# Low parts of every second mixer weight by an adding DMA in SBUF, with larger background budgets

## Chip, cores and metric

One core of a Trainium2 chip runs the kernel. The metric is the device time of one execution in microseconds (us), from runs without a profile; one more execution was profiled.

## What is computed

Two layers over 272 tokens (16 learned meta tokens and 256 inputs) of width 1024, all in float32:

```python
for l in range(DEPTH):
    h = h + 0.5 * swiglu(rmsnorm(h, g_ffn1[l]), w1_gate[l], w1_up[l], w1_down[l])
    n = rmsnorm(h, g_mix[l])
    z = n @ w_in[l]                      # u, q, k, v, f_logit, gates
    y_a = s5_mixer(u, ...)               # state space branch: a scan over time, 32 groups of 64 states
    y_b = forgetting_attention(q, k, v, f_logit + b_f[l])
    merged = gates[..., :D_MODEL] * (y_a @ w_br_a[l]) + gates[..., D_MODEL:] * (y_b @ w_br_b[l])
    h = h + merged @ w_o[l]
    h = h + 0.5 * swiglu(rmsnorm(h, g_ffn2[l]), w2_gate[l], w2_up[l], w2_down[l])
return rmsnorm(h[:, N_META:], g_final)
```

## The kernel before, in words

**Weights.** All weights stream from HBM once, as 378 units of 128 rows, most of them 1024 columns wide (512 KB). A product must keep float32's precision, so a weight w is split into a high part (w rounded to fp32r) and a low part (w minus the high part), and so is the activation. `unit` (L289 to L300) issues three matmuls for each of the 8 slices of a unit: high by high (L298), high by low activation (L299), low by high activation (L300). `load` (L138) issues the load from the SP queue into one of 4 `raw` buffers; `high` (L148) makes the high part on ScalarE (ACT) with the cast of L158, in one of 5 `wh` buffers; `low` (L162) makes the low part on VectorE (DVE) with the subtraction of L171, in one of 4 `wl` buffers.

**Order of the work.** The order on every engine is that in which the program issues instructions; nothing reorders it. `tick` (L264) is called after each unit. It calls `high` for the unit four ahead, then whatever is due (`due`: evictions, splits and copies registered with `later`), then `low` for the unit three ahead, then `background`. `group` (L302) does the first units of a stage a slice at a time and calls `high` and `low` inside. `background` (L252) runs a generator of small DVE operations, each with a price in the code's own nanoseconds, until the tick's budget is spent; a price that overshoots is paid back in the next ticks:

```python
state["credit"] = min(state["credit"], 0.0) + state["budget"]
while g is not None and (all_of_it or state["credit"] > 0):
    c = next(g, None)
    ...
        state["credit"] -= c
```

`finish_background` (L281) issues all that is left at once. In the first feed-forward block the generator is `ssm_setup` and `ssm_tables(0)` (the tables E and Cx, L601 to L633), begun 8 ticks into the block and finished at L1293 before the mixer starts; in the second one it is `ssm_tables(1)`; in a mixer it is `ssm_branch` (L638), finished at L1111.

**The mixer.** It takes 53 units, counted here from 0: units 0 to 3 give u, 4 (narrow, 256 columns) the forget gate, 5 to 8 v, 9 to 12 k, 13 to 16 q, 17 to 32 the gates with the attention between them, 33 and 34 the first half of the attention branch's projection, 35 to 38 the GLU of the state space branch, 39 to 44 the rest of both branches' projections, 45 to 52 the output projection. The budget is QKV_BUDGET in the ticks of units 0 to 16, GATE_BUDGET or LATE_BUDGET afterwards, FFN_BUDGET after L1111.

`have_u` (L757) scales a block of u, splits it and calls `done` (L761): 12 DMA copies from SBUF to SBUF, each of 32 rows and 34 KB, issued from the GpSimd (POOL) queue at L765, which lay the parts out for the matmul `bu` of the branch (L645). The ticks order them so: the copies of u's blocks 0 and 1 (24) are issued in the tick after unit 3, just ahead of `low` for unit 6; those of block 2 in the next tick, ahead of `low` for unit 7; those of block 3 in the one after, ahead of `low` for unit 8. The POOL queue holds these copies, the two memsets of L745 and little else. The state space branch's operations on DVE are products with the table E (L667), adds (L720, L722) and scans (L732); PE then forms the output with L657.

Of the kernel before, what the change touches and what calls it, by code (L numbers as in the profile page):

```python
# [7 lines left out]
F32 = mybir.dt.float32  # L8
F32R = mybir.dt.float32r
I32 = mybir.dt.int32  # L10
AF = mybir.ActivationFunctionType
ALU = mybir.AluOpType
# [4 lines left out]
D = 1024  # L17
KD = D // P
# [4 lines left out]
NF = DFF // P  # L23
DEPTH = 2
# [5 lines left out]
LEAD = 4  # L30
RAW = 4
SMALL = 200
FFN_BUDGET = 900.0
QKV_BUDGET = 1600.0
GATE_BUDGET = 2700.0
LATE_BUDGET = 2600.0
EARLY_B = 2
# [2 lines left out]
WARM = 10  # L40
START = 8
BLOCK = 1024
BROWS = 96
DELAY = 2
MASKED = -float(2.0 ** 100)
# [34 lines left out]
def plan():  # L80
    units = layer_units() * DEPTH
    blocks, where, off = [], [], 0
    for i, w in enumerate(units):
        if i > 4 and blocks and blocks[-1][1] + w <= BLOCK:
            blocks[-1][1] += w
        else:
            blocks.append([off, w])
        where.append((len(blocks) - 1, blocks[-1][1] - w, w))
        off += w
    return blocks, where, off  # L90


BLOCKS, WHERE, NCOL = plan()
# [36 lines left out]
class Weights:  # L130
# [7 lines left out]
    def load(self):  # L138
        if self.nb >= len(BLOCKS):
            return  # L140
        off, w = BLOCKS[self.nb]
        t = self.pool.tile([P, BLOCK], F32, tag="raw", name=f"raw{self.nb}", bufs=RAW)
        src = self.dram[off * P : (off + w) * P].rearrange("(p n) -> p n", p=P)
# [4 lines left out]
    def high(self, parts=1):  # L148
# [10 lines left out]
        self.part[i] = (hi, r)  # L159
        self.nh += 1  # L160

    def low(self, parts=1):  # L162
        i, nc = self.nl, self.nc
        if i >= len(WHERE):
            return
        w = WHERE[i][2]
        hi, r = self.part[i]
        lo = self.pool.tile([P, D], F32R, tag="wl", name=f"wl{i}", bufs=LEAD)
        for c in range(0, w, w // parts):
            k = slice(c, c + w // parts)  # L170
            nc.vector.tensor_sub(lo[:, k], r[:, k], hi[:, k].bitcast(F32))  # L171
        self.part[i] = (hi, lo)
        self.nl += 1
# [7 lines left out]
def body(tc, nc, ins, out):  # L181
    v, s, pe = nc.vector, nc.scalar, nc.tensor

    with (
# [49 lines left out]

        state = {"tick": 0, "bg": None, "credit": 0.0, "budget": FFN_BUDGET}
        queue, tails, mids = [], [], []
# [39 lines left out]
        def flush():  # L276
            due(10**9)
            while tails:
                tails.pop(0)()

        def finish_background():  # L281
            while state["bg"] is not None or mids:
                background(True)
                for fn in [mids.pop(0) for _ in range(len(mids))]:
                    fn()
                due(state["tick"] + 1)
# [26 lines left out]
        def split(hi, lo, x, then=None, when=None):  # L313
            s.copy(hi, x)  # L314

            def low():
                v.tensor_sub(lo, x, hi.bitcast(F32))
                if then is not None:
                    then()

            if when is None:
                later(1, low)
            else:
                when(low)


        def norm_in(d, gname, l, hh, hl, t0):

            x, g = h[:, d, t0:], pc(gname, l, d)
            a, b = hh(d)[:, t0:], hl(d)[:, t0:]  # L330
            s.activation(a, x, AF.Copy, scale=g)  # L331

            def low():
                v.scalar_tensor_tensor(b, x, g, a.bitcast(F32), ALU.mult, ALU.subtract)  # L334

            later(1, low)
# [197 lines left out]
        E = cp.tile([P, 2, NJ, TS + 1], F32, name="E")  # L534
        Bs = cp.tile([BROWS, NJ, 2 * P], F32R, name="Bs")
        Cx = cp.tile([P, 4, NJ, 32], F32, name="Cx")

        def ssm_tables(l):

            js = slice(l * NJ, (l + 1) * NJ)  # L540
            top = BROWS - 32
            for j in range(0, NJ, 4):
                x = Bs[:, j : j + 4].rearrange("p j c -> p (j c)")
                slots = halves.take(), halves.take(F32R)
                raw, hi = (y.rearrange("p a t -> p (a t)")[:BROWS, : 8 * P] for y in slots)
                nc.sync.dma_start(raw, ins["B"][l][:, j * 2 * P : (j + 4) * 2 * P])
# [91 lines left out]
        def ssm_branch(l, us, yr, t0):  # L638
            n = T - t0

            def bu(j):
                pb = bp.tile([P, 2, 512], F32, tag="b2", name=f"bu{next(names)}")
                m, q = divmod(j, 4)
                for r in range(2):
                    pe.matmul(pb[:, r, :T], lhsT=Bs[:, j, r * P : r * P + P], rhs=us[m](q)[:BROWS], start=True, stop=True)  # L645
                if q == 3:
# [94 lines left out]
        def mixer(l, hh, hl, t0, finish):  # L741
# [33 lines left out]
            state["bg"] = ssm_branch(l, us, yr, t0)  # L775
            state["budget"] = QKV_BUDGET
            for m in range(4):
# [333 lines left out]
            finish_background()  # L1111
            state["budget"] = FFN_BUDGET
            flush()
# [295 lines left out]
def _ssm_mats(inp):  # L1409
    B = np.zeros((DEPTH, 32, 4, 4, 2, P), np.float32)  # L1410
    C = np.zeros((DEPTH, P, 2, NJ, 32), np.float32)
    for r, (kb, kc) in enumerate((("ssm_b_re", "ssm_c_re"), ("ssm_b_im", "ssm_c_im"))):
        for gi in range(2):
# [3 lines left out]
            C[:, gi * 64 : gi * 64 + 64, r, :, gi * 16 : gi * 16 + 16] = c.transpose(0, 3, 1, 2)  # L1417
    return np.concatenate([B.reshape(DEPTH, 32, -1)] * (BROWS // 32), axis=1), C

# [27 lines left out]
```

## Time and profile before

| what | us |
|---|---|
| median of 3 runs (1238.59 to 1239.59) | 1239.27 |
| the profiled execution, whole | 1240.03 |
| its span, first to last instruction | 1238.2 |
| PE busy / DVE busy / ACT busy / POOL busy in the span | 1196.4 / 937.1 / 645.1 / 53.1 |

PE is TensorE's matmuls, PEld its weight loads, SPq the queue that issues the weight loads from HBM. "A <- B" behind a row's numbers names what ended a wait. Busy PE means that a matmul was in flight by modelled ends. PEclk is the granted TensorE clock, 1.00 for the upper of its two levels (2.4 GHz) and 0.50 for the lower (1.2 GHz). The first mixer lies at about 208 to 431 us of the span, the second at about 831 to 1040 us.

### The profile page before, as it was taken

What the parts mean: (1) busy time and instruction counts of PE and PEld (TensorE: products, weight loads), DVE (VectorE), ACT (ScalarE), POOL (GpSimd) and SP (SyncE); (2) the same over time, 40 slices, a digit from 0 to 9 for tenths busy, and PEclk for the clock granted to TensorE, in tenths of its full rate; (3) what the DMA queues carried; (4) which work ended last, traced back from release to release, by engine and by line L of the source; (5) the groups of instructions that cost most, each with busy time, mean ns of one, the idle gap of its engine ahead of it and who ended that gap; (6) DMA issues with size and microseconds to landing.
All of it is one profiled execution on the core that took longest, in us unless ns stands there. A gap on an engine that the chain in (4) does not pass through costs nothing.

```text
span 1238.2 us, 24127 instructions
## 1 busy us (share of the span) xinstructions
PE 1196.4 (97%) x9753; PEld 1170.0 (94%) x9753; DVE 937.1 (76%) x1722; ACT 645.1 (52%) x1052; POOL 53.1 (4%) x108
## 2 busy tenths in 40 slices
PE   9999999889979999999999999999999899999997
PEld 8999999788869999999999999999888699999997
DVE  7976888899997867888765555557998897756553
ACT  7556444536646665444454444446374576544542
POOL 0000000420000000000000000006100000000000
PEclk9999999899999999999999999999999899999999
DMA  7766554553334657655556555546432345655561
GB/s 243 208 194 202 183 176 137 171 160 116 93 99 133 188 179 228 181 175 166 174 171 185 178 172 166 176 156 207 154 103 87 102 154 172 225 185 186 175 186 64
DMA packets 60159, 204.71 MB, mean 165 GB/s; under 512 B 7920, under 2 KB 8304, under 8 KB 60048
## 3 DMA queue, kind: packets, MB, share of 16 engines
q1 hardware_dynamic: 56480, 199.06, 51.7%
q0 software_dynamic: 3152, 3.50, 0.9%
q8 instruction: 76, 1.25, 0.4%
q10 hardware_dynamic: 416, 0.62, 0.1%
q14 instruction: 35, 0.29, 0.1%
HBM read 198.75 MB, written 1.05 MB: 161 GB/s over the span
## 4 chain that ended last, share of the span: by engine, by line
PE 88%; DVE 9%; issue 2%; DMA 1%; ACT 0%; SPq 0%; DVEq 0%; ACTq 0%
PE ps L298 28%; PE ps L300 28%; PE ps L299 28%; DVE wl L171 2%; PE ps L657 2%; DVE m L667 1%; DVE g L732 1%; DVE p L667 1%; PE bu L645 1%; DMA raw<-wts 1%; PE ps L965 0%; DVE p L722 0%; DVE p L720 0%; PE ps L1030 0%; DVE mx L975 0%
## 5 line engine op out<-in xcount | busy, mean ns | idle before, releaser
L300 PE MATMUL ps<-m,wl 128*128 128x272 f32 (+2 forms) x2960 | 851.8, 288 | 6.3 <-DVE wl L171 6.3
L298 PE MATMUL ps<-m,wh 128*128 128x272 f32 (+2 forms) x2960 | 855.4, 289 | 0.8 <-ACT m L1064 0.5
L299 PE MATMUL ps<-m,wh 128*128 128x272 f32 (+2 forms) x2960 | 848.8, 287 | 0.1
L158 ACT CAST wh<-raw 128x1024 fp32r<-128x1024 f32 (+2 forms) x380 | 388.5, 1025 | 428.0 <-issue 222.5
L300 PEld LDWEIGHTS ps<-m,wl 128*128 128x128 f32 (+1 forms) x2960 | 558.8, 189 | 7.2 <-DVE wl L171 7.0
L298 PEld LDWEIGHTS ps<-m,wh 128*128 128x128 f32 (+1 forms) x2960 | 558.9, 189 | 5.6 <-issue 3.6
L299 PEld LDWEIGHTS ps<-m,wh 128*128 128x128 f32 (+1 forms) x2960 | 558.6, 189 | 1.0 <-DVE m L334 0.5
L171 DVE TENSOR_TENSOR wl<-raw,wh 128x1024 fp32r<-128x1024 f32 (+2 forms) x380 | 450.3, 1186 | 55.1 <-PE ps L300 38.9
L391 DVE TENSOR_TENSOR t<-t,ps 128x272 f32<-128x272 f32 (+1 forms) x88 | 38.1, 433 | 78.6 <-PE ps L300 76.2
L385 DVE TENSOR_TENSOR t<-ps,rstd 128x272 f32<-128x272 f32 (+1 forms) x88 | 38.3, 436 | 47.7 <-PE ps L300 47.2
L765 POOL DMA_DIRECT2D m<-m x96 | 47.2, 497 | 47.3 <-ACT m L314 32.9
L667 DVE TENSOR_TENSOR p<-bu,E 128x544 f32<-128x544 f32 x64 | 44.0, 720 | 4.0 <-PE bu L645 1.8
L667 DVE TENSOR_TENSOR m<-g,E 128x544 f32<-128x544 f32 x64 | 45.8, 719 | 0.1
L732 DVE TENSOR_TENSOR_SCAN g<-ssm_mag,p 128x272 f32<-128x272 f32 x64 | 43.5, 713 | 0.9
L393 ACT CAST m<-t 128x272 fp32r<-128x272 f32 (+1 forms) x88 | 36.2, 411 | 11.4 <-DVE t L391 11.3
L396 DVE TENSOR_TENSOR m<-t,m 128x272 fp32r<-128x272 f32 (+1 forms) x88 | 38.0, 432 | 3.7 <-ACT m L393 3.7
L419 DVE TENSOR_TENSOR t<-ps,rstd 128x272 f32<-128x272 f32 (+1 forms) x32 | 14.0, 438 | 34.6 <-PE ps L300 34.3
L386 ACT ACTIVATE t<-t 128x272 f32<-128x272 f32 (+1 forms) x88 | 37.2, 422 | 4.2 <-DVE t L385 4.0
L745 POOL MEMSET m<- 128x1088 f32 x4 | 4.0, 1008 | 770.3 <-PE ps L300 770.3
L657 PE MATMUL ps<-m,Cx 128*32 128x136 f32 (+3 forms) x384 | 22.5, 355 | 13.3 <-DVE m L667 13.3
L657 PEld LDWEIGHTS ps<-m,Cx 128*32 128x32 f32 x384 | 13.0, 120 | 19.2 <-DVE m L667 15.8
L331 ACT ACTIVATE m<-h,par 128x272 fp32r<-128x272 f32 (+1 forms) x48 | 24.5, 518 | 12.2 <-DVE h L421 7.2
(218 smaller groups left out, 685.9 us busy)
## 6 DMA issues: line engine op xcount, KB each, us to landing
raw<-wts SPq DMA_DIRECT2D x344, 512.0 KB, 3.6
raw<-wts SPq DMA_DIRECT2D x32, 384.0 KB, 3.2
m<-m POOLq DMA_DIRECT2D x96, 34.0 KB, 4.0
m<-B SPq DMA_DIRECT2D x8, 384.0 KB, 5.2
h<-hT SPq DMA_DIRECT2D x4, 272.0 KB, 5.2
m<-C SPq DMA_DIRECT2D x2, 512.0 KB, 4.6
out<-m SPq DMA_DIRECT2D x2, 256.0 KB, 2.1
out<-m ACTq DMA_DIRECT2D x1, 512.0 KB, 2.8
```

The source lines that it names most:

```text
L158: nc.scalar.copy(hi[:, c : c + w // parts], r[:, c : c + w // parts])
L171: nc.vector.tensor_sub(lo[:, k], r[:, k], hi[:, k].bitcast(F32))
L298: pe.matmul(ps[:width, :n], lhsT=a, rhs=mh, start=first and i == ks[0], stop=False)
L299: pe.matmul(ps[:width, :n], lhsT=a, rhs=ml, start=False, stop=False)
L300: pe.matmul(ps[:width, :n], lhsT=b, rhs=mh, start=False, stop=last and i == ks[-1])
L385: v.tensor_mul(x[:, :n], pg[:, :n], rstd[:, t0:])
L391: v.tensor_mul(y[:, :n], y[:, :n], pu[:, :n])
L396: v.tensor_sub(al(f)[:, t0:], y[:, :n], ah(f)[:, t0:].bitcast(F32))
L657: pe.matmul(ps[32 * q : 32 * q + 32, a - t0 : b - t0], lhsT=Cx[:, x, 4 * m + q, :], rhs=qt[q][:, row, a:b], start=start, stop=stop,)
L667: v.tensor_tensor(d[:, :, :, a : a + TS], x[:, :, a : a + TS].unsqueeze(1).to_broadcast([P, 2, 2, TS]), tab.unsqueeze(2).to_broadcast([P, ...
L732: v.tensor_tensor_scan(g[:, r], mg, p[:, r], 0.0, ALU.mult, ALU.add)
L765: nc.gpsimd.dma_start(x(q)[32 * i : 32 * i + 32].bitcast(F32), part(m)[32 * q : 32 * q + 32].bitcast(F32))
```

## The change

Within a layer's 189 units, those with an even number from 69 to 110 and 1024 columns, which are mixer units 2, 6, 8, 10 and so on to 42 (20 in each layer, 40 of 378), get their low part in another way: ACT writes the negated high part into the `wl` buffer, and a DMA issued from the POOL queue adds the raw weight to it in SBUF (512 KB). All other low parts stay on DVE. Two budgets grow.

```diff
-FFN_BUDGET = 900.0
-QKV_BUDGET = 1600.0
+FFN_BUDGET = 1000.0
+QKV_BUDGET = 1800.0
...
+DMA_LOW = (2 * NF + 3 * KD + 1, 2 * NF + 3 * KD + 43)
...
+    @staticmethod
+    def by_dma(i):
+
+        i %= len(WHERE) // DEPTH
+        return DMA_LOW[0] <= i < DMA_LOW[1] and i % 2 == 0 and WHERE[i][2] == D
+
     def low(self, parts=1):
...
         lo = self.pool.tile([P, D], F32R, tag="wl", name=f"wl{i}", bufs=LEAD)
-        for c in range(0, w, w // parts):
+        if self.by_dma(i):
+            nc.scalar.activation(lo[:, :w], hi[:, :w].bitcast(F32), AF.Copy, scale=-1.0)
+            nc.gpsimd.dma_start(lo[:, :w], r, accum_op=ALU.add)
+            parts = 0
+        for c in range(0, w, w // parts) if parts else ():
             k = slice(c, c + w // parts)
             nc.vector.tensor_sub(lo[:, k], r[:, k], hi[:, k].bitcast(F32))
```

## Rows read from the trace of the kernel before

**Rows 1.** The page, part 1: busy time by engine.

```profile
PE 1196.4 (97%) x9753; PEld 1170.0 (94%) x9753; DVE 937.1 (76%) x1722; ACT 645.1 (52%) x1052; POOL 53.1 (4%) x108
```

**Rows 2.** Waits of PE over the span: us in total, times, longest.

```profile
PE ps L657 <- DVE m L667: 13.3, 4, 4.5
```

**Rows 3.** The page, part 5: count, busy us, mean ns, idle before.

```profile
L158 ACT CAST wh<-raw 128x1024 fp32r<-128x1024 f32 (+2 forms) x380 | 388.5, 1025 | 428.0 <-issue 222.5
...
L171 DVE TENSOR_TENSOR wl<-raw,wh 128x1024 fp32r<-128x1024 f32 (+2 forms) x380 | 450.3, 1186 | 55.1 <-PE ps L300 38.9
```

**Rows 4.** Timeline where the first mixer starts: start, us, engine, line.

```profile
211.16 0.42 DVE L609 TENSOR_TENSOR vn<-E,s_a 128x256 f32<-128x256 f32 x1
...
215.48 0.17 DVE L579 TENSOR_TENSOR s_dt<-s_n 128x16 f32<-128x16 f32 x1
...
224.04 0.59 PE L300 MATMUL ps<-m,wl 128*128 128x272 f32 x1 [5.88 <-DVE wl L171]
```

**Rows 5.** Windows: PE, PEld, DVE, ACT, POOL busy (count), PEclk, DMA share, GB/s.

```profile
224.10:227.10 3.00, 3.00 (x13) 3.00 (x14) 3.00 (x5) 0.69 (x2) 0.00 (x0) 0.50 0.59 168
227.20:230.20 3.00, 3.00 (x26) 2.73 (x26) 3.00 (x6) 1.47 (x2) 2.13 (x5) 1.00 0.83 211
...
241.50:372.10 130.60, 116.64 (x1028) 106.95 (x1030) 124.69 (x220) 69.86 (x154) 13.47 (x28) 0.98 0.41 119
372.10:377.30 5.20, 5.20 (x48) 3.68 (x49) 1.09 (x3) 0.82 (x3) 0.00 (x0) 0.50 0.17 67
857.40:985.00 127.60, 115.50 (x991) 104.80 (x989) 117.83 (x204) 65.34 (x146) 12.25 (x25) 0.96 0.36 119
...
985.00:988.30 3.30, 3.30 (x42) 2.25 (x42) 3.06 (x7) 2.99 (x4) 0.00 (x0) 0.50 0.00 0
```

**Rows 6.** Timeline of DVE in the tick after mixer unit 3.

```profile
227.78 0.78 DVE L317 TENSOR_TENSOR m<-m,m 128x272 fp32r<-128x272 f32 x2
...
228.83 1.21 DVE L171 TENSOR_TENSOR wl<-raw,wh 128x1024 fp32r<-128x1024 f32 x1
```

**Rows 7.** Timeline of POOL: copies of L765 in both mixers.

```profile
227.12 0.51 POOL L765 DMA_DIRECT2D m<-m  x1 [19.93 <-ACT m L314]
...
242.22 1.47 POOL L765 DMA_DIRECT2D m<-m  x3
...
257.65 0.98 POOL L765 DMA_DIRECT2D m<-m  x2
...
841.80 0.50 POOL L765 DMA_DIRECT2D m<-m  x1 [13.00 <-ACT m L314]
...
870.83 0.98 POOL L765 DMA_DIRECT2D m<-m  x2
```

**Rows 8.** Timeline of PE: first L300 of unit 6, then of unit 8 twice.

```profile
234.88 0.29 PE L300 MATMUL ps<-m,wl 128*128 128x272 f32 x1
...
241.52 0.28 PE L300 MATMUL ps<-m,wl 128*128 128x272 f32 x1
...
857.40 0.28 PE L300 MATMUL ps<-m,wl 128*128 128x272 f32 x1
```

**Rows 9.** Issue to landing at L765, at L144; the page, part 3: weight queue.

```profile
DMA to landing us min/median/max: 1.7/4.0/6.2
...
DMA to landing us min/median/max: 2.0/3.6/8.3
...
q1 hardware_dynamic: 56480, 199.06, 51.7%
```

**Rows 10.** Timeline of ACT and PE around the first use of unit 42, both mixers.

```profile
392.15 1.99 ACT L158 CAST wh<-raw 128x1024 fp32r<-128x1024 f32 x2
...
397.96 0.29 PE L300 MATMUL ps<-m,wl 128*128 128x272 f32 x1
...
1003.54 1.99 ACT L158 CAST wh<-raw 128x1024 fp32r<-128x1024 f32 x2
...
1008.66 0.28 PE L300 MATMUL ps<-m,wl 128*128 128x256 f32 x1
```

## Prediction, made before the changed kernel ran

> **What bounds the kernel now.** I read the busy times first, then PE's waits, then windows over the mixers, last the timelines of POOL and PE. PE is busy in 1196.4 of 1238.2 us [rows 1], so nothing can give back more than 42 us, and the feed-forward blocks hold hardly any of it. What is idle lies in the mixers. The longest waits there are L657's, the state space branch's output, for DVE's products with the table: 13.3 us in 4 waits [rows 2]. Between the first low product of unit 8 and the end of those waits, DVE is busy in 124.7 of 130.6 us in the first mixer and in 117.8 of 127.6 us in the second, PE in 116.6 and 115.5 [rows 5]. So DVE ends last there, by a little: PE is idle for 14.0 and 12.1 us. That is what less work on DVE can win, however much work it is. A third place is the start of the first mixer, where PE waits 5.88 us for a low part that stands on DVE behind the last tables [rows 4].
>
> **The feed-forward budget.** In the first block the generator holds 70 steps of 200 and tables of 42,369, by the prices in the code, and gets 61 ticks. At 900 a tick, 33 operations are left for the end; the trace has just these, from 211.16 us. At 1000 the same count leaves 19, beginning with the fifth last small one at 215.48 us [rows 4]. The tail is 4.3 us shorter, and the wait of 5.88 us falls to about 1.6. After it PE ran at a granted clock of 0.50: 13 matmuls begin in 3.0 us, against 26 in the next 3.0 us at 1.00 [rows 5], which cost 1.5 us. So PE enters the mixer 5.8 us earlier, DVE and POOL 4.3 us. In the other blocks PE has no wait to lose: nothing.
>
> **The QKV budget** moves the branch's work on DVE forward: by the same count it ends in the tick of unit 33 in place of that of unit 34. It makes no work. I cost it at nothing; the DVE time below covers it.
>
> **DVE** loses 40 subtractions of 1.19 us [rows 3], 47 us in all, some 14 of them in each mixer's bound stretch (17 us). That exceeds the idle 14.0 and 12.1 us, so PE ends last afterwards and these are won, no more.
>
> **ACT** gets 40 negated copies. The cast of the same shape takes 1.03 us [rows 3], 41 us in all; ACT is busy 645.1 us [rows 1], 69.9 of 130.6 in the stretch [rows 5]. The copy waits until PE has left the unit four before, as the cast ahead of it in the tick already does. Behind it stand the next cast and evictions, a microsecond later. Nothing on the path, except late in the mixer (below).
>
> **The weight queue on SP.** A raw buffer is free only when the adding DMA has landed, so the load four blocks on starts that much later, and those behind it. It needs 3.6 us [rows 9]; the cast is issued four units ahead, 11 us at 26 matmuls in 3.0 us and 24 in a unit [rows 5], so I count nothing.
>
> **How long the adding DMA takes** the trace does not show. Low end: 1.7 us, the fastest copy from POOL; high end: 8.3 us, the slowest weight load of the same size [rows 9], and 10 if adding is slower than any copy. The nearest row is POOL's copy inside SBUF, median 4.0 us. It has 32 rows, the adding DMA 128 rows of 4 KB, 8 for each of 16 DMA engines, read twice (source and destination). A weight packet took 0.517 x 16 x 1238.2 / 56480 = 0.18 us, so 16 of them take 2.9 us, less 0.4 for what the small copy already has: 6.5 us. I take that.
> The Trainium skill (DMA: Bandwidth & Descriptors, section on the anatomy of one DMA on the SWDGE path) gives 2.0 us plus bytes over 436 GB/s, an estimate of 3.2 us for 512 KB. For POOL's 34 KB it would give 2.1, where the trace has a median of 4.0 [rows 9], so the trace speaks against it; by it the sum below would be +3.9 us, not +16.6.
>
> **The POOL queue** decides. The two L317 that finish the splits of u's blocks 0 and 1, and so their 24 copies, stand ahead of the low part of unit 6 [rows 6]: in the changed kernel its DMA stands behind 24 copies, that of unit 8 behind 48. Today a low part passes them by on DVE. Copies 22 to 24 run at 242.22 to 243.7 us, after PE has used unit 6's low part at 234.88 [rows 7, 8]. So PE waits at unit 6, and again at unit 8, whose DMA alone sets the end of both waits:
> - First mixer: the 48th copy ends at 257.65 + 0.98 = 258.6; 4.3 earlier, plus one more issue of 0.5: 254.8; landing at 261.3. PE used it at 241.52 [rows 8]: 19.8 us late.
> - Second mixer: 870.83 + 0.98 + 0.5 = 872.3; landing at 878.8, used at 857.40: 21.4 us late.
> Behind unit 6's DMA on POOL stand the copies of blocks 2 and 3, half a microsecond later, needed much later. DVE waits too, as the branch's first product comes from a matmul inside unit 6; with 17 us less to do it catches up before PE does.
>
> **The stages after.** PE then has 116.6 and 115.5 us of work, at its own pace. Each restart costs 1.5 us at the half clock, as above. The half-clock stretches after today's waits go: 372.1 to 377.3 (half of 5.2, 2.6 us), and in the second mixer 985 to 988.3 (1.6) and part of the mean of 0.96 over 127.6 us (5.1, of which I take 3.4, the rest being idle anyway) [rows 5].
> - First mixer: 19.8 + 1.5 - 14.0 - 2.6 = +4.7.
> - Second: 21.4 + 1.5 - 12.1 - 5.0 = +5.8.
> - Units 38 to 42 run at the full pace of PE. The cast ahead of unit 42's copy ends at 393.2 (half of the two casts from 392.15), the copy at 394.2, landing at 400.7; PE wants it at 397.96: 2.7 us. In the second mixer 1004.5, 1005.6, 1012.1 against 1008.66: 3.4 us [rows 10]. I count the last of each chain, since an earlier wait gives time to the next: +6.1.
>
> Sum: +16.6 on 1240.0 of the profiled execution. That stood 0.8 above the median, so **1256** for the median.
>
> **Rivals.**
> 1. *The queue drains quickly* (faster). With PE stopped, weight loads stand still, and POOL's copies may go at their bare issue of 0.49 us, without the gaps in between. Then unit 8's DMA starts at 222.8 + 48 x 0.49 + 0.5 = 246.8, lands 4.0 later at 250.8, 9.3 late, and the first mixer comes to -5.8. The second: 841.80 + 24.0 + 4.0 = 869.8, 12.4 late, -3.2. Late units 1.1. Sum -7.9: 1231. It decides from the point where both landings come some 5.3 us before mine. For it: 31.5 us for 48 copies is well over 23.5 [rows 7]. Against it: the gaps are waits for the copies' own landings.
> 2. *The two cancel*: landings some 5 us earlier, 1239.
> 3. *Adding is slow*, 10 us: 3.5 us more at unit 8, and at each of three units at PE's pace late in the mixer (2 x 4 x 3.5 = 28): 1284. For it: each element is read twice and added. Against it: no row.
> 4. *The adding DMA does not stand behind the copies*, the change thus not doing what its place in the program says. Then the lateness goes, and -5.8 - 14.0 - 2.6 - 12.1 - 5.0 + 6.1 = -33: 1206. Against it: POOL's copies run in the program's order today.
>
> **Chances.** Forecast 0.57, slow adding 0.15, quick queue 0.14, cancelling 0.10, not behind the copies 0.04. About 0.2% is what a measurement can tell from no change: faster by more 0.18, within it 0.10, slower 0.72. The range takes in the forecast's own bounds (6.5 less 4 and plus 2), most of the quick queue and slow adding: 1233 to 1280.
>
> **What would show it.** Right: the wait at L300 for a POOL DMA of 10 us or more at unit 6 and 5 or more at unit 8 in both mixers, the clock at 0.50 behind them; POOL's copies unbroken before them; DVE idle in the same stretch, and L657's waits for DVE gone; the wait at the first mixer's start near 1.6 us; ACT's new line near 1.03 us. Wrong: unit 6's DMA issued before the copies, landings near 2 us, waits of L657 on DVE as long as before, or PE waiting all through the gates for adding DMAs.

## The result and the profile after

The changed kernel takes **1269.85 us** (median of 4 runs, 1266.69 to 1274.59) against 1239.43 us for the kernel before on the same chip: a ratio of **1.0248, 95% interval 1.0214 to 1.0281**, slower by 30.4 us. The forecast was 1256, its range 1233 to 1280. The profiled execution took 1266.69 us, its span (first to last instruction) 1264.9, 26.7 more than the 1238.2 of before. All lines of the code behind the new function stand 11 numbers higher: L300 is now L311, L171 L182, L657 L668, L667 L678, L765 L776; the adding DMA is L178, the negated copy L177.

The page of the changed kernel, parts 1, 2 (the slices of POOL), 5 and 6:

```profile
span 1264.9 us, 24220 instructions
PE 1202.2 (95%) x9753; PEld 1178.7 (93%) x9753; DVE 894.1 (71%) x1682; ACT 682.9 (54%) x1092; POOL 88.0 (7%) x148
...
POOL 0000000710010000000000000008000000000000
...
L182 DVE TENSOR_TENSOR wl<-raw,wh 128x1024 fp32r<-128x1024 f32 (+2 forms) x340 | 401.8, 1182 | 60.0 <-PE ps L311 41.3
L178 POOL DMA_DIRECT2D wl<-raw x40 | 34.9, 882 | 912.5 <-ACT wl L177 781.5
...
wl<-raw POOLq DMA_DIRECT2D x40, 512.0 KB, 5.3
```

DVE lost its 40 subtractions: 340 are left of 380 [rows 3], and it is busy 43 us less than in [rows 1]. PE's idle time went the other way, from 41.8 to 62.7 us. The other 5.8 us of the span are PE's own: 1202.2 us busy against 1196.4 for the same 9753 matmuls, at a mean granted clock of 0.975 against 0.986. Where PE was idle, its waits over the span say (us in total, times, longest):

```profile
PE ps L311 <- DMA wl<-raw: 45.8, 11, 14.0
PE ps L668 <- DVE m L678: 1.7, 2, 1.1
...
PE ps L311 <- DVE wl L182: 1.3, 2, 1.1
```

The wait for DVE's products fell from 13.3 us [rows 2] to 1.7, and the one at the first mixer's start from 5.88 [rows 4] to 1.1. In their place stand eleven waits for the adding DMA, 45.8 us. The six longest of them, in PE's timeline (start, us, engine, line; idle time before and what ended it in brackets), are those at units 6, 8, 36 and 40 of the first mixer and at 6 and 8 of the second.

```profile
243.22 0.60 PE L311 MATMUL ps<-m,wl 128*128 128x272 f32 x1 [14.04 <-DMA wl<-raw]
...
257.40 0.59 PE L311 MATMUL ps<-m,wl 128*128 128x272 f32 x1 [4.59 <-DMA wl<-raw]
...
385.00 0.39 PE L311 MATMUL ps<-m,wl 128*128 128x272 f32 x1 [3.40 <-DMA wl<-raw]
...
403.02 0.60 PE L311 MATMUL ps<-m,wl 128*128 128x272 f32 x1 [3.41 <-DMA wl<-raw]
...
874.45 0.59 PE L311 MATMUL ps<-m,wl 128*128 128x272 f32 x1 [9.81 <-DMA wl<-raw]
...
887.96 0.59 PE L311 MATMUL ps<-m,wl 128*128 128x272 f32 x1 [3.81 <-DMA wl<-raw]
```

The rows of units 6 and 8 are to be compared with [rows 8]. Why PE waits there is seen on POOL. Its timeline in the first mixer:

```profile
222.61 0.53 POOL L776 DMA_DIRECT2D m<-m  x1 [11.11 <-ACT m L325]
223.98 3.91 POOL L776 DMA_DIRECT2D m<-m  x8 [0.85 <-DVE m L328]
229.02 1.47 POOL L776 DMA_DIRECT2D m<-m  x3 [1.13 <-DMA m<-m]
230.74 4.43 POOL L776 DMA_DIRECT2D m<-m  x9 [0.25 <-issue]
236.20 1.59 POOL L776 DMA_DIRECT2D m<-m  x3 [1.02 <-DMA m<-m]
238.04 0.91 POOL L178 DMA_DIRECT2D wl<-raw  x1 [0.25 <-issue]
...
251.05 1.49 POOL L776 DMA_DIRECT2D m<-m  x3 [0.16 <-issue]
252.75 1.83 POOL L178 DMA_DIRECT2D wl<-raw  x2 [0.21 <-issue]
```

The first 24 copies end at 237.79 us (236.20 + 1.59), and only then, at 238.04, is unit 6's DMA issued; 24 more follow, and unit 8's is issued at 252.75. POOL goes through its queue in the program's order, as the copies do in [rows 7], and PE starts 0.04 us after each landing (243.18 and 257.36 us).

Windows of the changed kernel, with the columns of [rows 5]: the wait at unit 6, the stretches that answer to 241.50:372.10 and 857.40:985.00, and three late in the mixers.

```profile
228.90:243.20 14.30, 0.27 (x3) 0.05 (x1) 1.23 (x1) 8.01 (x14) 11.74 (x23) 0.60 0.63 156
257.40:375.60 118.20, 116.52 (x1017) 108.64 (x1019) 97.57 (x183) 74.41 (x156) 10.33 (x12) 0.98 0.68 174
384.95:388.70 3.75, 3.70 (x17) 3.71 (x18) 0.00 (x0) 1.46 (x4) 0.08 (x1) 0.54 0.91 157
402.98:409.20 6.22, 6.17 (x27) 6.18 (x28) 2.03 (x6) 0.99 (x2) 0.85 (x1) 0.50 0.79 205
887.90:1003.00 115.10, 111.95 (x982) 103.94 (x985) 96.68 (x178) 73.21 (x152) 10.33 (x12) 0.97 0.66 179
...
1026.90:1030.40 3.50, 3.50 (x18) 3.50 (x18) 0.91 (x3) 0.89 (x1) 0.86 (x1) 0.51 0.72 212
```

In the first row POOL is busy 11.74 of 14.30 us while DVE has 1.23 us of work: the copies hold up PE and DVE alike. In the second PE is busy 116.52 of 118.20 us, and DVE 97.57: PE has become the bound there. The late rows are stretches behind a wait, with the granted clock near 0.50.

### The profile page after: what moved, and what is told of

Read it like the earlier page. It is cut to its first block, busy times and chain, and to the rows that moved or that the text cites. A ratio compares the mean times of both kernels' runs of the same rounds, so it can differ in the third digit from the quotient of the medians.

```text
span 1264.9 us, 24220 instructions
## 1 busy us (share of the span) xinstructions
PE 1202.2 (95%) x9753; PEld 1178.7 (93%) x9753; DVE 894.1 (71%) x1682; ACT 682.9 (54%) x1092; POOL 88.0 (7%) x148
## 3 DMA queue, kind: packets, MB, share of 16 engines
q0 software_dynamic: 8912, 24.47, 10.1%
HBM read 198.75 MB, written 1.05 MB: 158 GB/s over the span
## 4 chain that ended last, share of the span: by engine, by line
PE 81%; DVE 7%; DMA 5%; issue 3%; POOL 2%; ACT 1%; SPq 0%; DVEq 0%; POOLq 0%; ACTq 0%
PE ps L311 26%; PE ps L309 26%; PE ps L310 25%; DMA wl<-raw 3%; POOL m L776 2%; DMA raw<-wts 1%; DVE wl L182 1%; DVE g L743 1%; DMA m<-m 1%; DVE m L678 1%; DVE p L678 1%; PE ps L668 1%; PE ps L976 1%; PE bu L656 0%; DVE p L731 0%
## 5 line engine op out<-in xcount | busy, mean ns | idle before, releaser
L311 PE MATMUL ps<-m,wl 128*128 128x272 f32 (+2 forms) x2960 | 858.0, 290 | 47.2 <-DMA wl<-raw 45.8
L309 PE MATMUL ps<-m,wh 128*128 128x272 f32 (+2 forms) x2960 | 860.0, 291 | 0.4 <-ACT wh L159 0.4
L159 ACT CAST wh<-raw 128x1024 fp32r<-128x1024 f32 (+2 forms) x380 | 388.9, 1024 | 446.7 <-issue 211.5
L311 PEld LDWEIGHTS ps<-m,wl 128*128 128x128 f32 (+1 forms) x2960 | 563.4, 190 | 50.8 <-DMA wl<-raw 48.3
L309 PEld LDWEIGHTS ps<-m,wh 128*128 128x128 f32 (+1 forms) x2960 | 563.5, 190 | 5.4 <-issue 3.3
L182 DVE TENSOR_TENSOR wl<-raw,wh 128x1024 fp32r<-128x1024 f32 (+2 forms) x340 | 401.8, 1182 | 60.0 <-PE ps L311 41.3
L178 POOL DMA_DIRECT2D wl<-raw x40 | 34.9, 882 | 912.5 <-ACT wl L177 781.5
L678 DVE TENSOR_TENSOR p<-bu,E 128x544 f32<-128x544 f32 x64 | 44.3, 721 | 46.1 <-PE bu L656 43.6
L776 POOL DMA_DIRECT2D m<-m x96 | 47.8, 548 | 26.5 <-ACT m L325 18.5
L678 DVE TENSOR_TENSOR m<-g,E 128x544 f32<-128x544 f32 x64 | 45.9, 718 | 0.1
L404 ACT CAST m<-t 128x272 fp32r<-128x272 f32 (+1 forms) x88 | 36.2, 411 | 13.6 <-DVE t L402 13.4
L177 ACT ACTIVATE wl<-wh 128x1024 fp32r<-128x1024 f32 x40 | 42.1, 1052 | 0.0
L345 DVE SCALAR_TENSOR_TENSOR m<-h,par,m 128x272 fp32r<-128x272 f32 (+1 forms) x48 | 23.4, 494 | 8.3 <-ACT m L342 8.2
```

The costliest lines, as they stand in the source:

```text
L159: nc.scalar.copy(hi[:, c : c + w // parts], r[:, c : c + w // parts])
L177: nc.scalar.activation(lo[:, :w], hi[:, :w].bitcast(F32), AF.Copy, scale=-1.0)
L309: pe.matmul(ps[:width, :n], lhsT=a, rhs=mh, start=first and i == ks[0], stop=False)
L311: pe.matmul(ps[:width, :n], lhsT=b, rhs=mh, start=False, stop=last and i == ks[-1])
L678: v.tensor_tensor(d[:, :, :, a : a + TS], x[:, :, a : a + TS].unsqueeze(1).to_broadcast([P, 2, 2, TS]), tab.unsqueeze(2).to_broadcast([P, ...
L776: nc.gpsimd.dma_start(x(q)[32 * i : 32 * i + 32].bitcast(F32), part(m)[32 * q : 32 * q + 32].bitcast(F32))
```

## The experiments

Two theories stood against each other. **A**: the time is lost where POOL's copies stand ahead of the adding DMAs (units 6 and 8) and in the late units, and nothing else takes the place of either wait when it goes. **B**: it is the adding DMA as such, its duration and the buffers it holds, at any unit. With each median stands its ratio to the kernel before, which took 1239.16 to 1239.96 us beside these runs, and the ratio's 95% interval. The range's first mixer unit is what is added to `2 * NF + 3 * KD`, plus 1; only even units count.

**The early units out** (units 10 to 42 by DMA):

```diff
-DMA_LOW = (2 * NF + 3 * KD + 1, 2 * NF + 3 * KD + 43)
+DMA_LOW = (2 * NF + 3 * KD + 9, 2 * NF + 3 * KD + 43)
```

> Units 2, 6 and 8 of each mixer get their low part on DVE again; 10 to 42 keep the adding DMA, budgets as changed. Theory A (the POOL queue holds the DMAs of units 6 and 8 behind the copies of u): PE's waits of 14.0 + 4.7 us and 9.8 + 3.9 us go and are not replaced, since DVE has less work; in the trace of the changed kernel PE passed unit 8 some 15.9 us later than before in the first mixer. Without that it leaves unit 34 some 18 us earlier than before (5.8 from the front, 12 of DVE waits) and the second mixer some 12 us earlier; the waits of units 36 to 42 stay. 1233 us, 1225 to 1242. Theory B (adding DMAs land too late wherever they stand in the u to q stage, since the DMA engines are busy): the waits move on to units 10 to 16 and the time stays above 1258 us.

Measured: 1256.57 us (1249.53 to 1256.94), 1.0121 (1.0094 to 1.0148). Neither number. In the profiled execution, the fastest of the four (1249.53), PE still waits 35.6 us for adding DMAs in 10 waits, the longest 12.5.

**The late units out** (units 2 to 32):

```diff
-DMA_LOW = (2 * NF + 3 * KD + 1, 2 * NF + 3 * KD + 43)
+DMA_LOW = (2 * NF + 3 * KD + 1, 2 * NF + 3 * KD + 34)
```

> Units 34 to 42 get their low part on DVE again; 2 to 32 keep the adding DMA, budgets as changed. Theory A (late in the mixer PE takes a unit every 3 us, and copy, issue and landing take longer than the three units they have; each wait then costs half clock too): from unit 34 on 11.0 and 8.7 us come back: 1250 us, 1245 to 1256; waits at units 6 and 8 as they were. Rival (DVE or the high parts are late there as well, and the wait only changes its name): 1262 us or more.

Measured: 1253.35 us (1252.62 to 1254.15), 1.0109 (1.0094 to 1.0124), as A says. The units from 34 on cost 16.5 us, well over the 6.1 that the prediction has for them.

**Both out** (units 10 to 32):

```diff
-DMA_LOW = (2 * NF + 3 * KD + 1, 2 * NF + 3 * KD + 43)
+DMA_LOW = (2 * NF + 3 * KD + 9, 2 * NF + 3 * KD + 34)
```

> Both cuts: only units 10 to 32 get the adding DMA, budgets as changed. Theory A: the two effects add, as they lie in different stretches: 1213 us, 1204 to 1224, faster than the kernel before. Theory B: 1250 us or more.

Measured: 1240.13 us (1237.08 to 1242.93, 10 runs), 1.0005 (0.9995 to 1.0016). Theory A's range missed by 16 us, theory B's bound by 10. POOL's and PE's timelines of this kernel, then its waits of PE, tell why:

```profile
250.23 1.47 POOL L776 DMA_DIRECT2D m<-m  x3 [0.56 <-DMA m<-m]
251.73 1.86 POOL L178 DMA_DIRECT2D wl<-raw  x2
...
256.43 0.59 PE L311 MATMUL ps<-m,wl 128*128 128x272 f32 x1 [13.31 <-DMA wl<-raw]
```

```profile
PE ps L311 <- DMA wl<-raw: 24.1, 2, 13.3
PE ps L668 <- DVE m L678: 7.0, 2, 4.1
```

The queue theory was right and its place incomplete. Without the waits at units 6 and 8, PE comes to unit 10 while POOL is still at the 48 copies; its DMA stands behind them until 251.73, and the wait moves there, 13.31 us in the first mixer and the rest of the 24.1 us in the second. PE waits for no other adding DMA in that run. The first experiment missed for the same reason: there unit 10's DMA is issued at 251.45 us, behind the 48 copies.

**The budgets alone** (the kernel before, with the two budgets of the change):

```diff
-FFN_BUDGET = 900.0
-QKV_BUDGET = 1600.0
+FFN_BUDGET = 1000.0
+QKV_BUDGET = 1800.0
```

> The kernel before with FFN_BUDGET 1000 and QKV_BUDGET 1800 and no adding DMA. By the prediction's term the wait at the first mixer's start falls from 5.88 to 1.6 us and the half clock after it goes: 5.8 us of PE, 4.3 us of DVE, which ends last in the first mixer: 1235 us, 1233 to 1236. Rival (the front gain is given back, since DVE only reaches the same last wait): 1238 to 1241 us.

Measured: 1232.84 us (1231.10 to 1234.01), 0.9942 (0.9927 to 0.9957). The budgets alone make the kernel 7.1 us faster; the whole change takes 37 us longer than they do.

**Only units that come to PE after the copies** (units 14 to 32):

```diff
-DMA_LOW = (2 * NF + 3 * KD + 1, 2 * NF + 3 * KD + 43)
+DMA_LOW = (2 * NF + 3 * KD + 13, 2 * NF + 3 * KD + 34)
```

> Units 14 to 32 alone get the adding DMA, budgets as changed. In the run from unit 10 the wait had only moved: unit 10 stood behind all 48 copies (POOL free at 251.7 and 868.1 us) and PE waited 13.3 and 10.8 us. Theory A (queue): POOL is free some 5 us before unit 14 needs its part, so no wait for an adding DMA over 1.5 us is left in the u to q stage, and DVE has 10 subtractions less in each mixer (12 us), about what PE waits for it with the budgets alone (21 us in all): 1216 us, 1210 to 1224. Theory B (the first adding DMA of a mixer waits wherever it stands, from engines or rings): a wait of 10 us or more at unit 14 in both mixers, 1236 us or more.

Measured: **1219.46 us** (1218.76 to 1220.05), 0.9840 (0.9826 to 0.9855), as the repaired theory A says; theory B expected 1236 us or more. From the page (part 6), then PE's two largest waits of this kernel in total:

```profile
wl<-raw POOLq DMA_DIRECT2D x20, 512.0 KB, 4.8
```

```profile
PE bu L656 <- issue: 7.9, 6, 2.3
PE ps L668 <- DVE m L678: 7.1, 2, 4.1
```

Against the budgets alone it is 13.4 us faster. These two waits were 11.9 and 9.0 us there, so they explain 5.9 us of it; PE's own busy time fell by 7.8 us, from 1197.7 to 1189.9. PE's waits have none for an adding DMA. Taken in this order, the runs divide the whole change into four parts: budgets -6.6 (against 1239.43), units 14 to 32 -13.4, units 2 to 12 +33.9 (1253.35 less 1219.46), units 34 to 42 +16.5. In another order the last part is the same: 1256.57 less 1240.13 is 16.4.

**The copies on another queue** (units 2 to 32, the copies of L776 issued from SP):

```diff
-DMA_LOW = (2 * NF + 3 * KD + 1, 2 * NF + 3 * KD + 43)
+DMA_LOW = (2 * NF + 3 * KD + 1, 2 * NF + 3 * KD + 34)
...
-                            nc.gpsimd.dma_start(
+                            nc.sync.dma_start(
```

> Units 2 to 32 with the adding DMA as in the run to unit 32 (1253 us), but the 96 copies of u are issued from SP's queue in place of POOL's. Theory A (what units 6 and 8 wait for is POOL's queue and nothing else): the adding DMAs of 6 and 8 are issued within 2 us of their negated copies, the waits of 14.0 + 4.7 and 9.8 + 3.9 us and most of the half clock behind them go: 1214 us, 1206 to 1226. Theory B (the DMA engines are full in that stage): the waits stay over 5 us and the time over 1240 us. Rival: SP, with 48 issues of 0.33 us and their waits for DVE among the weight loads, makes high parts late: waits at L309 for the cast, 1225 to 1245 us.

Measured: 1263.77 us (1261.50 to 1264.47), 1.0192 (1.0175 to 1.0209), worse than with the copies on POOL. Timelines of POOL, SP and ACT, then the waits of ACT and of PE in this kernel:

```profile
226.13 0.87 POOL L178 DMA_DIRECT2D wl<-raw  x1 [14.61 <-ACT wl L177]
234.77 0.88 POOL L178 DMA_DIRECT2D wl<-raw  x1 [7.78 <-ACT wl L177]
...
227.27 18.22 SPq L776 DMA_DIRECT2D m<-m  x24
245.59 0.53 SPq L145 DMA_DIRECT2D raw<-wts  x1
...
249.75 1.04 ACT L159 CAST wh<-raw 128x1024 fp32r<-128x1024 f32 x1 [14.12 <-DMA raw<-wts]
```

```profile
ACT wh L159 <- DMA raw<-wts: 104.8, 38, 14.1
...
PE ps L870 <- ACT P L864: 30.6, 6, 7.5
PE ps L311 <- DMA wl<-raw: 6.5, 5, 3.1
```

The queue's part is settled: units 6 and 8 have their DMAs issued at 226.13 and 234.77, as soon as ACT's copy is done, 12 and 18 us earlier than in the changed kernel, and all waits for adding DMAs together are 6.5 us. The time was lost elsewhere. SP now issues 96 copies between weight loads, so loads come late: 24 copies hold SP for 18.22 us, and only then is the next load issued, at 245.59. ACT's casts wait 104.8 us for loads, and the copies of L864 behind them on ACT come late to PE, which waits 30.6 us for them. The rival named this cause, but it expected PE's waits at L309 and at most 1245 us.

**Unit 8 without unit 6** (units 8 to 42, a single execution):

```diff
-DMA_LOW = (2 * NF + 3 * KD + 1, 2 * NF + 3 * KD + 43)
+DMA_LOW = (2 * NF + 3 * KD + 7, 2 * NF + 3 * KD + 43)
```

> Units 8 to 42 with the adding DMA, so only unit 6 goes back to DVE. Theory A (unit 8's DMA, behind 48 copies, sets the end of both waits): PE waits some 18 us at unit 8 in the first mixer and 13 in the second, and uses its low part at 257 us of the span in the first mixer, within 1.5 us of the changed kernel's 257.4; total within 4 us of the changed kernel's. Rival (each wait costs for itself): unit 8's part is used at 243 us and 25 us come back.

Measured: 1267.09 us. PE's timeline in the first mixer, then in the second:

```profile
255.78 0.59 PE L311 MATMUL ps<-m,wl 128*128 128x272 f32 x1 [19.08 <-DMA wl<-raw]
...
887.85 0.60 PE L311 MATMUL ps<-m,wl 128*128 128x272 f32 x1 [16.26 <-DMA wl<-raw]
```

One wait of 19.08 us in place of 14.04 and 4.59, ended at 255.78 against 257.40, and one of 16.26 in place of 9.81 and 3.81, ended at 887.85 against 887.96: unit 8's DMA alone sets the end of both waits, as the prediction has it. The first end is 1.6 us sooner, where 1.5 was allowed, and the second wait longer than the 13 us expected.

**Copying without adding** (all 40 units; what it leaves out stands in its expectation):

```diff
-            nc.gpsimd.dma_start(lo[:, :w], r, accum_op=ALU.add)
+            nc.gpsimd.dma_start(lo[:, :w], r)
```

> As changed, but the DMA copies the raw weight over the negated high part and does not add: the low parts of 40 units are thus the weights themselves, so the computation differs. Theory (adding reads its destination too, as the prediction's 2.9 us assumed, of which half would go): median issue to landing falls from 5.3 us by 1 us or more, and the waits at units 36 to 42 shrink by 1 us each. Rival (adding costs nothing over a copy of the same rows): median within 0.4 us of 5.3, waits as in the changed kernel.

Measured: 1250.64 us, a single execution. Issue to landing (min, median, max) of L178, in the changed kernel first and then in this one, and then this one's waits of PE:

```profile
DMA to landing us min/median/max: 4.5/5.3/8.8
```

```profile
DMA to landing us min/median/max: 2.8/3.4/6.8
```

```profile
PE ps L311 <- DMA wl<-raw: 34.2, 9, 11.1
```

The addition costs 1.9 us of the DMA's median, and 0.33 us of POOL at each issue (0.86 against 0.53 us). The long waits stay: 34.2 of 45.8 us. But the addition is no small part of the loss: without it the span is 1248.9 us, 16.0 shorter than the changed kernel's, 11.6 of it in these waits. In the late units (36 to 42) they fall from 6.8 to 3.6 us in the first mixer and from 6.2 to 3.9 in the second, though not each by 1 us: unit 42 of the first mixer, without a wait in the changed kernel, has 2.5 us here.

**The feed-forward budget alone** (the kernel before with one line changed):

```diff
-FFN_BUDGET = 900.0
+FFN_BUDGET = 1000.0
```

> The kernel before with FFN_BUDGET 1000 and nothing else. By the prediction all that the budgets win is the front (5.8 us) and QKV_BUDGET is worth nothing: 1233.5 us, as with both budgets (1232.8) within 1.5 us. Rival (the QKV budget wins the rest, as the branch's work starts earlier on a DVE that ends last): 1236 us or more.

Measured: 1234.79 us (1233.21 to 1235.75), 0.9959 (0.9946 to 0.9973), 4.4 us faster than the kernel before. The QKV budget is thus worth some 2 us more or nothing: this interval and that of both budgets overlap.

**More units by DMA** (units 14 to 32 and the odd units 19 to 33):

```diff
-DMA_LOW = (2 * NF + 3 * KD + 1, 2 * NF + 3 * KD + 43)
+DMA_LOW = (2 * NF + 3 * KD + 13, 2 * NF + 3 * KD + 34)
...
-        return DMA_LOW[0] <= i < DMA_LOW[1] and i % 2 == 0 and WHERE[i][2] == D
+        return DMA_LOW[0] <= i < DMA_LOW[1] and (i % 2 == 0 or i >= 2 * NF + 3 * KD + 18) and WHERE[i][2] == D
```

> As the run of units 14 to 32, and the odd units 19 to 31 by adding DMA too (17 units in each mixer, was 10). Theory (DVE still ends last there: in that run PE waits 7.1 us in L668 for DVE's products and 7.9 us in the branch's first product; the gates' units have 3.5 to 9 us between landing and use): 7 subtractions less, 8 us of DVE in each mixer, take the 7.1 us and part of the 7.9: 1210 us, 1206 to 1215. Rival (DVE is not what ends last any more, or two adding DMAs in a row land too late): 1217 us or more.

Measured: 1225.85 us (1221.85 to 1226.52), 0.9882 (0.9866 to 0.9899), 6.4 us slower than every second unit. The rival's number held, for another reason than the two it gives: PE waits 6.0 us for DVE in L668, against 7.1, and 1.5 us for adding DMAs. The trace has 36 of these, 18 in each mixer, one more than the expectation counts. The waits of ACT, first in this kernel, then with units 14 to 32 alone:

```profile
ACT wh L159 <- DMA raw<-wts: 68.7, 37, 7.3
```

```profile
ACT wh L159 <- DMA raw<-wts: 26.7, 24, 5.5
```

Each adding DMA holds its raw buffer until it has landed, so the load into that buffer starts later: SP waits 183.5 us for adding DMAs before its loads, against 121.2 with units 14 to 32 alone. With one at nearly every unit the casts wait 68.7 us for loads, and loads have 3.3% of the chain of work that ended last, against 0.8% with units 14 to 32 alone. The same wait was 15.3 us (longest 2.0) in the kernel before and 39.6 (longest 7.3) in the changed one.

**A larger feed-forward budget**, on that kernel and on the one with units 14 to 32:

```diff
-FFN_BUDGET = 1000.0
+FFN_BUDGET = 1100.0
```

> As the run before, with FFN_BUDGET 1100: by the count of prices 2 operations instead of 19 are left at the end of the first feed-forward block, 6 us of DVE. Theory (PE's remaining wait of about 1.1 us there goes, and DVE starts the first mixer 6 us earlier): 2 to 6 us below the run before. Rival (DVE has no room left in the feed-forward block, so its evictions come late and PE waits there): not below it.

> Units 14 to 32 by adding DMA as in the fastest run, with FFN_BUDGET 1100. If the front is additive, as it was in the pair with all gates by DMA (2.5 us), 1217 us, 1215 to 1219. Rival (the wait at unit 14 or DVE's tail takes it back): 1219 to 1221.

Measured: 1223.38 us (1222.57 to 1224.06), 2.5 less than without it; and **1215.59 us** (1215.43 to 1217.12), 0.9801 (0.9785 to 0.9817), 3.9 less. The second is the fastest version measured, 24 us under the kernel before. The head of its page:

```profile
span 1213.8 us, 24183 instructions
PE 1186.6 (98%) x9753; PEld 1164.1 (96%) x9753; DVE 914.9 (75%) x1702; ACT 664.0 (55%) x1072; POOL 70.9 (6%) x128
```

PE is idle for 27.2 us, and its own busy time is 15.6 us under the changed kernel's for the same 9753 matmuls, with a mean granted clock of 0.996 against 0.975.

A longer lead, with weights fetched and split five units ahead in place of four, may give late DMAs more room. It was not tried.

## Why the prediction was right, and where it was off

The direction and the main mechanism were right: the DMAs of units 6 and 8 wait behind 24 and 48 copies, DVE's bound goes, PE ends last. The waits at units 6 and 8 are 14.04 and 4.59 us, and 9.81 and 3.81 in the second mixer, where the signs of being right asked for 10 and 5. The size fell short, +16.6 us against +26.7 in the two spans, and errors of opposite sign hide a part of that (the last paragraph of this section). By its steps:

- **Feed-forward budget.** Forecast -5.8 us, the wait of 5.88 down to 1.6. Measured alone -4.4, the wait down to 1.1. Right, a little high.
- **QKV budget.** Costed at nothing; there are some -2 us between the runs with both budgets and with one, which their intervals do not tell from nothing.
- **DVE and ACT.** L668's waits are down to 1.7 us, DVE is off the path; the negated copy takes 1052 ns, forecast 1.03 us. Right. What the copies do to ACT's other work is under the late units. Of L668's wait 7.0 and 7.1 us stay where the units from 34 on are left to DVE (units 2 to 32, units 14 to 32).
- **The adding DMA's duration.** Forecast 6.5 us, measured 5.3 in the median and 4.6 at both units 8. A little too long. I let the trace's 34 KB copies (median 4.0) speak against the Trainium skill (DMA: Bandwidth & Descriptors, the SWDGE anatomy), by which 512 KB are an estimate of 3.2 us. The plain copy came near it, with 3.4; the addition took 1.9 us more. The median of 4.0 was no fixed price of a small copy: the same copies have 2.8 us in the changed kernel and 3.6 with units 14 to 32 alone. What lengthened them no run shows.
- **The POOL queue.** Unit 8's part came at 257.40, forecast 261.3: 15.9 us late for 19.8. In the second mixer, with the 14.0 us by which it starts later taken off, 16.6 for 21.4. So 4 to 5 us too much each. In the first mixer POOL came to it 1.6 us sooner (252.75 for 254.3), and it landed 4.6 us after its issue began, forecast 7.0 with the issue. From there to the start of unit 35 the mixers gained less than forecast, 12.9 and 12.6 us for 15.1 and 15.6. The end of both waits is set by unit 8 alone, as the run without unit 6 shows.
- **After unit 8.** PE starts unit 35 at 378.83 us, before at 375.81: +3.0, forecast +4.7. In the second mixer +4.0, forecast +5.8. A little high, and near in part by luck: unit 8's part came 3.9 and 4.8 us sooner than forecast, but the stretch behind it gained less.
- **The late units: the term that failed.** "I count the last of each chain, since an earlier wait gives time to the next: +6.1." From the start of unit 35 to that of unit 53 the mixers took 11.0 and 8.7 us longer than before, 19.7 in all; taking these units out brought 16.5. Unit 42, the only one of them that was priced, waits not at all in the first mixer and 1.1 us in the second, forecast 2.7 and 3.4. Three things were left out. First, an earlier wait did not spare the next: in the second mixer there are four. PE's waits of the changed kernel from 1010 to 1066 us, then windows with the columns of [rows 5], of the kernel before from the start of unit 35 on, of the changed kernel around the first of these waits, and behind that wait:

```profile
PE ps L311 <- DMA wl<-raw: 6.2, 4, 2.1
```

```profile
988.30:1009.00 20.70, 20.70 (x174) 20.56 (x174) 17.20 (x35) 16.24 (x33) 0.00 (x0) 1.00 0.53 168
...
1003.30:1026.90 23.60, 17.48 (x168) 16.13 (x166) 15.56 (x35) 22.39 (x39) 2.60 (x3) 1.00 0.74 191
1011.17:1014.17 3.00, 3.00 (x25) 3.00 (x26) 0.06 (x1) 2.83 (x6) 0.86 (x1) 1.00 0.87 277
```

  ACT had no time to catch up in. From 1003.30 to 1026.90 it was busy in 22.39 of 23.60 us and waited for PE nowhere, so a stop of PE brought no copy forward. Unit 42's cast ended 19.5 us after PE began unit 35, before 16.1; three negated copies, of units 36, 38 and 40, have joined ACT's work ahead of it, 1.05 us each, and the prediction let the casts come as before. In the first mixer one cast there waited 3.0 us for PE, so there a stop of PE did hold back the chain after it. No run took work off ACT late in the mixers, so how much of the waits this makes stays open. Second, I looked at unit 42 alone, though my own third rival counts three late units in each mixer; in the first mixer the waits come at units 36 and 40 (3.4 us each). Third, the half clock behind three of these six waits: 17 and 27 matmuls in 3.75 and 6.22 us where, at 26 in 3.0 us [rows 5], 2.0 and 3.1 would do, and 18 in 3.50 us in the second mixer where 2.1 would: 6.3 us. Behind the wait of 2.12 us at 1011.17 the clock stayed at 1.00. With the waits themselves, 6.8 us in the first mixer and 6.2 in the second, that is 19.3 of the 19.7. And I gave these DMAs one duration, 6.5 us; the eight of units 36 to 42 took 5.4 to 8.8, 7.0 in the mean, at a DMA share of 0.77 in 1006.40 to 1040.00 us.
- **Raw buffers.** Costed at nothing. In the changed kernel ACT's waits for loads grew by 24 us, and the chain of work that ended last has a load late in each mixer: 6.55 us from 379.38 and 4.50 from 1015.37. Loads have 1.4% of that chain, before 0.5%, and 3.3% with a DMA at nearly every unit. The cover I named, the issue of the cast four units ahead, was thin.
- **"Not behind the copies", 1206 us.** The units whose DMAs do stand clear of the copies and of the late mixer give 1219.46, not -33 but -20: only half the DMAs are left, and DVE's waits with them in part.
- **The other rivals.** The queue did not drain quickly: 48 copies took from 222.61 to 252.54 us, 29.9, where that rival has 23.5, and 27.4 in the second mixer. The second rival's landings, some 5 us earlier than mine, nearly came (3.9 and 4.8), but not its 1239 us, for the late units. Adding took 5.3 us in the median, not 10, though the landings of up to 8.8 us did late in the mixers a part of what that rival says.

Up to unit 35 the forecast was 3.5 us too high (10.5 for 7.0 in the two mixers), after it 13.6 too low (6.1 for 19.7): the 10.1 us between the two spans' forecast and measured difference. A further 3.2 us lie between the profiled execution, the fastest of the four, and the median of 1269.85.

## What to carry to other kernels

When work moves from an engine to a DMA, list what stands ahead of it in the queue that issues it, in program order, and compare the issue time with the first use, unit by unit; where a long batch is ahead, the first unit to take is the one that its consumer reaches after the batch, not merely after the first late one. At the pace of a bound engine a chain of cast, copy and DMA has to end ahead of its use with its slowest landing, not its median, and a miss can be paid twice, as a wait and as a half clock behind it: here behind seven of eleven waits. The engine that now starts the chain needs room of its own: ACT, busy in 54% of the whole span, had none just where the units came fastest. An operation that reads a buffer longer delays that buffer's next load too, so take half of the units and measure before taking all.

## What the runs showed of the hardware that was not expected

An adding DMA inside SBUF costs more at both ends than a copy of the same 512 KB: 5.3 against 3.4 us from issue to landing in the median, and 0.86 against 0.53 us of POOL at the issue. Landings ranged from 4.5 to 8.8 us in one run. The eight of units 36 to 42 took 5.4 to 8.8, but unit 10 and unit 16 of both mixers and unit 18 of the first took 7.4 to 8.4 too, and no run shows what makes one long. A wait of PE did not always leave the half clock behind it: after one of 2.12 us (1011.17) 25 matmuls began in 3.0 us at 1.00, after one of 2.07 (1026.70) the clock was 0.51. Copies inside SBUF issued from SP rather than POOL were no cheaper for the kernel: 1263.77 against 1253.35 us with the same units by DMA, through the weight loads behind them.
